# A DiT block on one core: the Fourier output product's sums and splits on VectorE and ScalarE, ordered behind the heads on both, and a quarter of the first sums on TensorE

## The chip, the cores and the metric

The kernel runs on one core of a Trainium2 chip. The metric is the device time of one execution in microseconds; lower is better. The core has five engines that each work through their own queue in order: PE (TensorE, matmuls), DVE (VectorE), ACT (ScalarE), POOL (GpSimd) and SP (SyncE, which here only starts DMAs). They meet at semaphores.

## The reference

One block of a diffusion transformer over 2048 tokens of width 1024, with 256 context tokens. What matters here, cut from the reference:

```python
m = jax.nn.silu(cond) @ w + b                       # ada_mod: six rows of modulation
hx = modulate(rms_norm(x, norm1_g[l]), sh1, sc1)
fx, qx, kx, vx = split_projection(hx @ w_in[l])
y_four = fourier_mix(fx)                            # real part of a 2-D FFT, 4 groups of 128
y_attn = neighbourhood_attention(qx, kx, vx, kc, vc, rpb[l])   # 8 heads
gates = jax.nn.sigmoid(h @ w_gate)
merged = g_f * (y_four @ w_fo) + g_a * (y_attn @ w_ao)
x = x + g1 * (merged @ w_o)
x = x + g2 * sqrelu_mlp(hx2, w_mlp1[l], w_mlp2[l])
```

The two places of the change are `silu(c) @ w_ada` for the first modulation, and `y_four @ w_fo`, the Fourier output product.

## The kernel before, in words

The program runs in stages, and most of them hand over by data: first the modulation sums and the first product of the input projection (to about 80 us of the profile), the rest of the projections (to about 835 us), the Fourier transforms (838 to 893), the attention heads (893 to 1230), the merge and output projection, and the MLP (1510 to the end).

**First stage.** For each of eight groups of 128 channels (k), `ada_sum` (L255) multiplies weight slices by silu(c) on DVE and adds them up in two accumulators; `ada_cols` (L268) then sums over partitions on TensorE with single-column matmuls: slices that DVE left are multiplied directly (L275), DVE's sum against ones (L276). PE_K (L605) says how many of the eight slices DVE takes for k = 2 and later; k = 0 and 1 are wholly DVE's. The result scales the tokens' channel group, which feeds the matmuls `ps_first`.

**Splits.** Matmuls that need more than one rounding take each operand as a high part and a low part: `split_on(eng_lo, hi, lo, src, eng_hi)` (L81) copies the source to `hi` on ACT, or on `eng_hi` where one is given (L85), and subtracts it from the source on `eng_lo` (L86).

**Heads.** There are 128 head steps: 4 head pairs (hp), 4 row blocks (rb), 4 column blocks (cb), 2 heads (h2). `block` (L1138) is one step: score matmuls `sc` (L1155, L1158), bias and minimum on DVE (L1164, output `s`, `m`), exponential on ACT (L1168), transposes `tp` on PE (L1177), high part `pH` on ACT (L1180), low part `pL` on DVE (L1185), matmuls `pv` (L1191) and their copy `yp` (L1194). Three steps are in flight, one stage apart. `behind("pe")`, `behind("dve")` and `behind("act")` keep each of these behind the last head instruction of its engine.

**Beside the heads** runs the generator `merge_fourier` (L1024 on), which computes y_four @ w_fo. It is pulled once or twice a step, under `issue_after(last_qk)` and `behind("dve")`; a scheduler then places its instructions by a model of when they are ready. In it: `load_w` fetches weight rows `wf` and their mirror `wm` (for half p = 0 on SP, for p = 1 on POOL's queue); the spectrum halves are fetched from DRAM `yF`; for each p the sum `ws` (POOL, L1055) and the difference `wf` (DVE, L1056) are made and split into wpH/wpL, wdH/wdL, and the spectrum into yaH/yaL, ybH/ybL (high parts on DVE, low parts on POOL but for wpL). Then the 4 rows at frequency 64 are loaded into `s64`, copied to `w64` and `a64` on ACT (L1076), and their low parts subtracted on POOL (L1078). The row product `pr` (L1092) of 14 matmuls is copied to `row`, turned by the transposes `puc` (L1098) and copied to `uc`. After that come 208 matmuls `pmf` (L1115), summed on DVE into `mo` (L1124, L1125) and stored. `pr`, `puc`, `pmf` and the transposes `ty` of the heads share one PSUM buffer. The generator goes on with the loads for the attention output product.

Of the kernel before, what the change touches and what calls it, by code (L numbers as in the profile page):

```python
# [8 lines left out]
F32 = mybir.dt.float32  # L9
# [5 lines left out]
ALU = mybir.AluOpType  # L15
# [44 lines left out]
def dit_block(ctx: ExitStack, tc: tile.TileContext, a, out, taps=None, upto=9):  # L60
# [42 lines left out]
    tT = [scratch(f"tT{c}", [16, 120, TCOL[c]]) for c in range(3)]  # L103


    yF = scratch("yF", [2, 2, 128, 1024])
    y64 = scratch("y64", [4, 1024])

    wfr = scratch("wfr", [4, 63, D])
# [492 lines left out]
    hx32 = [hx_room(f"first{o}").bitcast(F32R).rearrange("p o k t -> p (o k t)").rearrange("p (k t) -> p k t", t=512) for o in "HL"]  # L602
    first = [mmp.tile([128, 512], F32, tag="mm", name=f"ps_first{m}") for m in range(4)]
    sums, made = [], []
    PE_K = 4  # L605

    def first_sums(k):
        if k not in first_ada:
# [258 lines left out]
    def seq_dft(p):  # L867

        room = fb.tile([128, S], F32, tag="X", name="A1") if p else None
        for i in range(4):  # L870
            ps = seq_part(Gs[p][i], i, f"{p}_{i}")
            o = room[:, i * 512:(i + 1) * 512] if p else room_for(i, f"A{p}_{i}")
            if i == 0:
                add_alternating(o, ps, col[:, 2 * p:2 * p + 1])
            else:
                act.activation(o, ps, AF.Copy)
            act.dma_start(yF[p, i % 2, :, (i // 2) * 512:(i // 2 + 1) * 512], o)

    def seq_dft64():
        for i in (0, 2):  # L880
# [143 lines left out]
    def merge_fourier():  # L1024
# [14 lines left out]
        def load_w(p, fetch):  # L1039
# [5 lines left out]
                fetch(wm[o + 1:o + 64], wfr[2 * p + h])  # L1045
            return w, wm, t

        rows = load_w(0, fetch)
        for p in range(2):
            for x in range(2):  # L1050
                fetch(ys[x][1][:, p].bitcast(F32), yF[p, x])
        yield
        for p in range(2):
            w, wm, t = rows
            pool.tensor_tensor(t, w, wm, op=ALU.add)  # L1055
            dve.tensor_tensor(out=w, in0=w, in1=wm, op=ALU.subtract)  # L1056
            yield
            split_on(dve, ws[0][0][:, p], ws[0][1][:, p], t, dve)
            yield
            split_on(pool, ws[1][0][:, p], ws[1][1][:, p], w, dve)  # L1060
            if p == 0:
                rows = load_w(1, pool.dma_start)
            yield
            for x in range(2):
                hi, lo = (t[:, p] for t in ys[x])
                split_on(pool, hi, lo, lo.bitcast(F32), dve)
                yield

        w64, a64 = (mf.tile([68, D], F32R, tag=n, name=n) for n in ("w64", "a64"))
        c64 = mf.tile([68, 1], F32R, tag="c64", name="c64")  # L1070
        for r, src, lo in ((w64, raw(wf, 64 * D, [[128 * D, 4], [1, D]]), 64), (a64, y64, 32)):
            t = stage("s64", 68)
            pool.memset(t, 0.0)
            for o in (0, 32, 64):
                pool.dma_start(t[o:o + 4], src)
            act.activation(r, t, AF.Copy)  # L1076
            los = slice(lo, lo + 4)
            pool.tensor_tensor(r[los], t[los], r[los].bitcast(F32), op=ALU.subtract)  # L1078
# [23 lines left out]
        for m in range(8):  # L1102
            ms = slice(m * 128, (m + 1) * 128)
            o = [stage(f"mo{m}_{h}") for h in range(2)]
            pool.tensor_copy(o[1][:, 0:1], uc[:, m:m + 1])
            for par in range(2):
                ts = slice(par * 512, (par + 1) * 512)
                for x in range(2):
                    ps = mmp.tile([128, 512], F32, tag="mm", name=f"pmf{m}_{par}{x}")
                    (wH, wL), (yH, yL) = ws[x], ys[x]  # L1110
                    prods = [(l[:, p, ms], r[:, p, ts]) for p in range(2) for l, r in ((wH, yH), (wH, yL), (wL, yH))]
                    if x == 0:
                        prods.append((w64[:, ms], a64[:, ts]))
                    for i, (l, r) in enumerate(prods):
                        pe.matmul(ps, l, r, start=(i == 0), stop=(i == len(prods) - 1))  # L1115
                        count += 1
                        if count % 2 == 0 and i < len(prods) - 1:
                            yield
                    if x == 0:
                        u = mf.tile([128, 512], F32, tag="u", name=f"u{m}_{par}", bufs=2)  # L1120
                        act.activation(u, ps, AF.Copy)
                    else:
                        f = 1 - par
                        dve.tensor_tensor(out=view(o[0], par, [[2, 512]]), in0=u, in1=ps, op=ALU.subtract)  # L1124
                        dve.tensor_tensor(out=view(o[1], 1022 + par, [[-2, 512 - f]]), in0=u[:, f:], in1=ps[:, f:],  # L1125
                                          op=ALU.add)
                    if count % 2 == 0:
# [500 lines left out]
```

## Time and profile before

| | |
|---|---|
| median of 3 runs | 2784.8 us (2781.84 to 2786.85) |
| profiled execution | 2787.32 us |
| its span in the profile | 2785.5 us |
| granted TensorE clock, mean | 0.975 |
| PE busy | 2657.8 us (95%) |
| DVE, ACT, POOL busy | 1707.1, 1178.6, 371.2 us |
| chain that ended last | PE 77%, DVE 7%, DMA 7% |

All times below are on the clock of the profiled execution, from the start of its span. Busy time of PE contains the slowing by a lower granted clock; the mean of a group mixes it in. A row of the waits names what an engine waited for, in us. Instruction names leave buffer numbers out, so that w64 reads `w` and a64 reads `a`; a line can be that of a helper (L78, L85, L86).

### The profile page before, as it was taken

To read this page: it belongs to the slowest core of one execution; us is meant where nothing else is said; L and a number is where in the kernel's file an instruction comes from. 1 tells how busy PE (TensorE), PEld (TensorE's weight loads), DVE (VectorE), ACT (ScalarE), POOL (GpSimd) and SP (SyncE) were. 2 spreads that over 40 slices of the span, in tenths; PEclk is the share of its full clock that TensorE was granted. 3 is DMA by queue.
4 is the path that set the end of the run, shared out by engine and by line. 5 is a ranking of instruction groups with operands and counts; after the bars stand their busy time and mean duration, and the time that the engine had idled before them with its cause. 6 is when DMAs were issued, how large, how long until landed. Compare 5 with 4: busy or idle time off the path is not lost.

```text
span 2785.5 us, 41746 instructions
## 1 busy us (share of the span) xinstructions
PE 2657.8 (95%) x16257; PEld 1614.1 (58%) x16257; DVE 1707.1 (61%) x3366; ACT 1178.6 (42%) x2065; POOL 371.2 (13%) x496
## 2 busy tenths in 40 slices
PE   7899988999999699989999899999999999999999
PEld 6445656876647578878886344444444444444444
DVE  5656985255534768887666656655558456665536
ACT  4633226332323568863444644433333544433322
POOL 1111221012226745511000000000000000000000
PEclk8999999999998889999999999999999999999999
DMA  8487689452336455556656412111116211112102
GB/s 238 122 228 204 210 261 292 136 166 73 91 131 171 103 142 154 163 185 229 215 201 236 164 61 61 50 57 60 47 55 246 77 61 61 61 46 61 46 1 98
DMA packets 280862, 366.66 MB, mean 132 GB/s; under 512 B 38769, under 2 KB 217161, under 8 KB 276313
## 3 DMA queue, kind: packets, MB, share of 16 engines
q1 hardware_dynamic: 263913, 337.27, 38.7%
q0 software_dynamic: 11264, 16.76, 2.3%
q10 hardware_dynamic: 5488, 9.98, 1.0%
q8 instruction: 127, 2.08, 0.3%
q14 instruction: 70, 0.57, 0.1%
HBM read 277.83 MB, written 87.12 MB: 131 GB/s over the span
## 4 chain that ended last, share of the span: by engine, by line
PE 77%; DVE 7%; DMA 7%; ACT 1%; issue 1%; POOL 1%; SPq 0%; ACTq 0%; DVEq 0%; POOLq 0%
PE p L78 24%; PE pm L78 20%; PE ps_g L78 8%; PE po L78 6%; DMA w12m<-in_w_mlp 3%; PE pua L78 3%; PE ps_k L78 3%; PE tp L1177 2%; PE ps_v L78 2%; PE pv L1191 2%; PE pmf L1115 2%; PE sc L1155 1%; PE sc L1158 1%; DVE w1m L326 1%; DVE aaccg L264 1%
## 5 line engine op out<-in xcount | busy, mean ns | idle before, releaser
L78 PE MATMUL pm<-hc,wc 128*128 128x512 f16 x2688 | 589.1, 381 | 16.7 <-ACT p L1475 8.1
L78 PEld LDWEIGHTS <-wc 128*128 128x128 f16 x2688 | 264.2, 98 | 338.7 <-issue 25.6
L78 PE MATMUL p<-w2H,aH 128*128 128x512 f16 x1024 | 388.1, 379 | 0.5 <-ACT aH L1470 0.5
L78 PE MATMUL p<-w2H,aL 128*128 128x512 f16 x1024 | 388.1, 379 | 0.1
L78 PE MATMUL p<-w2L,aH 128*128 128x512 f16 x1024 | 388.1, 379 | 0.0
L1453 DVE TENSOR_TENSOR acc<-p,acc 128x512 f32<-128x512 f32 x224 | 154.7, 691 | 318.4 <-PE p L78 318.2
L78 PE MATMUL ps_g<-hx,w_g 128*128 128x512 f16 x1536 | 342.4, 380 | 0.7 <-ACT ot_f L419 0.7
L78 PEld LDWEIGHTS <-aH 128*128 128x128 f16 x2048 | 200.3, 98 | 242.2 <-ACT aH L1470 1.0
L1442 ACT ACTIVATE w2H<-w2s,msc 128x1024 f16<-128x1024 f32 x64 | 70.6, 1141 | 443.6 <-PE p L78 435.8
L78 PEld LDWEIGHTS <-w_g 128*128 128x128 f16 x1536 | 150.9, 99 | 171.3 <-issue 3.2
L78 PEld LDWEIGHTS <-hx 128*128 128x128 f16 x2304 | 226.1, 99 | 40.4 <-issue 6.7
L78 PEld LDWEIGHTS <-aL 128*128 128x128 f16 x1024 | 100.2, 98 | 121.3 <-DVE aL L1471 0.6
L947 POOL DMA_DIRECT2D bt<-tT x264 | 132.8, 510 | 66.0 <-DVE ri L1184 47.1
L1164 DVE CUSTOM_DVE_ANT_0 s<-sc,bt,qsc 128x736 f32<-128x736 f32 (+5 forms) x128 | 111.2, 869 | 44.8 <-PE sc L1158 40.3
L1443 DVE SCALAR_TENSOR_TENSOR w2L<-w2s,msc,w2H 128x1024 f16<-128x1024 f32 x64 | 80.7, 1282 | 92.6 <-ACT w2H L1442 92.6
L1442 ACT ACTIVATE wc<-ws,msc 128x512 f16<-128x512 f32 x128 | 91.1, 716 | 103.5 <-PE pm L78 101.5
L1185 DVE SCALAR_TENSOR_TENSOR pL<-tp,pH 128x640 f16<-128x640 f32 (+1 forms) x128 | 112.1, 876 | 24.5 <-ACT pH L1180 24.1
L419 ACT ACTIVATE ot_g<-ps_g,usc_g 128x512 f32<-128x512 f32 x64 | 43.7, 685 | 185.8 <-PE ps_g L78 180.6
L1168 ACT ACTIVATE s<-s,m 128x736 f32<-128x736 f32 (+5 forms) x128 | 104.4, 816 | 14.2 <-DVE m L1164 13.1
L78 PE MATMUL po<-wouH,mH 128*128 128x512 f32 x256 | 101.0, 398 | 7.2 <-DVE ga L1234 7.2
L1177 PE MATMUL tp<-ident,s 128*128 128x128 f32 x704 | 105.4, 285 | 2.2 <-ACT s L1168 2.2
L78 PE MATMUL po<-wouH,mL 128*128 128x512 f32 x256 | 100.5, 393 | 0.0
(494 smaller groups left out, 4724.1 us busy)
## 6 DMA issues: line engine op xcount, KB each, us to landing
w12m<-in_w_mlp SPq DMA_DIRECT2D x32, 1024.0 KB
w1r<-in_w_mlp SPq DMA_DIRECT2D x32, 1024.0 KB
w2s<-in_w_mlp SPq DMA_DIRECT2D x64, 512.0 KB
gT<-ot_g SPq DMA_DIRECT2D x64, 256.0 KB
hc<-hcd SPq DMA_DIRECT2D x14, 1024.0 KB
hcd<-ho SPq DMA_DIRECT2D x42, 256.0 KB
x<-in_x SPq DMA_DIRECT2D x20, 512.0 KB
ws_g<-in_w_branch_gate SPq DMA_DIRECT2D x16, 512.0 KB
```

Of the source, the lines that this page charges most:

```text
L78: last_mm[0] = pe.matmul(ps, l, r, start=(start and i == 0), stop=(stop and i == n - 1))
L419: act.activation(o, ps, func, scale=scale)
L947: load_(t[i * 16:(i + 1) * 16, :, off + j0 * w:off + (j0 + 8) * w], raw(tT[ct], (2 * hp * 15 + dr) * w, [[120 * w, 16], [15 * w, 2], [1, 8 ...
L1115: pe.matmul(ps, l, r, start=(i == 0), stop=(i == len(prods) - 1))
L1164: tail["dve"] = dve.tensor_tensor_reduce(out=s[:, :n], in0=sc, in1=bias, op0=ALU.add, op1=ALU.min, scale=qsc[:, 4:5], scalar=3.0e38, accum ...
L1168: tail["act"] = act.activation(s[:, :n], s[:, :n], AF.Exp, bias=m1[:, 0:1], scale=-1.0, accum_out=m1[:, 1:2])
L1177: tail["pe"] = pe.transpose(tp[:, i * 128:(i + 1) * 128], s[:, o:o + 128], ident)
L1185: tail["dve"] = dve.scalar_tensor_tensor(out=pL[:, :c], in0=tp[:, :c], scalar=PTOP, in1=pH[:, :c], op0=ALU.mult, op1=ALU.subtract)
L1191: tail["pe"] = pe.matmul(pv, p_[:nk, i * 128:(i + 1) * 128], vv[:nk, h2 * 128 + o:h2 * 128 + o + 64], start=(j == 0 and i == 0), stop=(j = ...
L1442: act.activation(hi, src, AF.Copy, scale=scale)
L1443: dve.scalar_tensor_tensor(out=lo, in0=src, scalar=scale, in1=hi, op0=ALU.mult, op1=ALU.subtract)
L1453: dve.tensor_tensor(out=o, in0=x, in1=y, op=ALU.add)
```

## The change

It has three parts.

1. PE_K goes from 4 to 6: for k = 2 to 7, DVE sums six of the eight weight slices, and TensorE multiplies two instead of four directly.
2. In the Fourier output product, the sum `ws` goes from POOL to DVE, all eight high parts of weights and spectrum go from DVE to ACT, all low parts that POOL made go to DVE, and so do the two low parts of w64 and a64. Differences stay on DVE. The s64 tiles are allocated, cleared and loaded at the start of the generator, in the buffers of `u`, which become 1024 columns wide. DRAM `yF` becomes four tensors.
3. The pulls of the generator stand behind the last head instruction on ACT too, not on DVE alone.

```diff
@@ yF
-    yF = scratch("yF", [2, 2, 128, 1024])
+    yF = [[scratch(f"yF{p}{x}", [128, 1024]) for x in range(2)] for p in range(2)]
@@ first stage
-    PE_K = 4
+    PE_K = 6
@@ merge_fourier
+        s64 = []
+        for src in (raw(wf, 64 * D, [[128 * D, 4], [1, D]]), y64):
+            t = mf.tile([68, D], F32, tag="u", name="s64", bufs=2)
+            pool.memset(t, 0.0)
+            for o in (0, 32, 64):
+                pool.dma_start(t[o:o + 4], src)
+            s64.append(t)
...
-            pool.tensor_tensor(t, w, wm, op=ALU.add)
+            dve.tensor_tensor(out=t, in0=w, in1=wm, op=ALU.add)
             dve.tensor_tensor(out=w, in0=w, in1=wm, op=ALU.subtract)
             yield
-            split_on(dve, ws[0][0][:, p], ws[0][1][:, p], t, dve)
-            yield
-            split_on(pool, ws[1][0][:, p], ws[1][1][:, p], w, dve)
+            split_on(dve, ws[0][0][:, p], ws[0][1][:, p], t)
             if p == 0:
                 rows = load_w(1, pool.dma_start)
             yield
+            split_on(dve, ws[1][0][:, p], ws[1][1][:, p], w)
+            yield
             for x in range(2):
                 hi, lo = (t[:, p] for t in ys[x])
-                split_on(pool, hi, lo, lo.bitcast(F32), dve)
+                split_on(dve, hi, lo, lo.bitcast(F32))
                 yield
...
-        for r, src, lo in ((w64, raw(wf, 64 * D, [[128 * D, 4], [1, D]]), 64), (a64, y64, 32)):
-            t = stage("s64", 68)
-            pool.memset(t, 0.0)
-            for o in (0, 32, 64):
-                pool.dma_start(t[o:o + 4], src)
+        for r, lo in ((w64, 64), (a64, 32)):
+            t = s64.pop(0)
             act.activation(r, t, AF.Copy)
             los = slice(lo, lo + 4)
-            pool.tensor_tensor(r[los], t[los], r[los].bitcast(F32), op=ALU.subtract)
+            dve.tensor_tensor(out=r[los], in0=t[los], in1=r[los].bitcast(F32), op=ALU.subtract)
             yield
...
-                        u = mf.tile([128, 512], F32, tag="u", name=f"u{m}_{par}", bufs=2)
+                        u = mf.tile([128, D], F32, tag="u", name=f"u{m}_{par}", bufs=2)[:, :512]
@@ step
-            with tc.issue_after(last_qk[0].ins), behind("dve"):
+            with tc.issue_after(last_qk[0].ins), behind("dve"), behind("act"):
                 next(filler, None)
```

The new lines move the numbering: what is line n before stands at n + 4 from the middle of the generator on (L1164 becomes L1168, L1092 becomes L1096). The scheduler places the instructions anew. Three places follow, each before and after.

**DVE, the second half (p = 1) of the weight sums.** Names end in row block and column block, so `s_..,m_3_2` is the score instruction of rb 3, cb 2. Before:

```order
L1164 ISA s_9102,m_3_2_10460<-sc_3_2_10455,bt_9001,qsc 128x640
L1164 ISA m_3_2_10460 128x1
L1184 RECIPROCAL ri_3_1_10462<-m_3_1_10366 128x1
L1056 TENSOR_TENSOR wf_9364<-wf_9364,wm_9365 128x1024
L85 CAST wpH<-ws_9366 128x1024
L85 CAST wdH<-wf_9364 128x1024
L86 TENSOR_TENSOR wpL<-ws_9366,wpH 128x1024
L1185 SCALAR_TENSOR_TENSOR pL_3_1_10453<-tp_3_1_10446,pH_3_1_10452 128x640
L1164 ISA s_9103,m_3_2_10509<-sc_3_2_10504,bt_9001,qsc 128x640
```

After (here rb 1, cb 2 and 3):

```order
L1188 RECIPROCAL ri_1_1_9683<-m_1_1_9588 128x1
L86 TENSOR_TENSOR yaL<-yaL,yaH 128x1024
L1063 TENSOR_TENSOR ws_9319<-wf_9317,wm_9318 128x1024
L1189 SCALAR_TENSOR_TENSOR pL_1_1_9674<-tp_1_1_9666,pH_1_1_9673 128x768
L1168 ISA s_9095,m_1_3_9731<-sc_1_3_9726,bt_8988,qsc 128x616
L1168 ISA m_1_3_9731 128x1
L1188 RECIPROCAL ri_1_2_9733<-m_1_2_9638 128x1
L86 TENSOR_TENSOR ybL<-ybL,ybH 128x1024
L1064 TENSOR_TENSOR wf_9317<-wf_9317,wm_9318 128x1024
L1189 SCALAR_TENSOR_TENSOR pL_1_2_9724<-tp_1_2_9716,pH_1_2_9723 128x768
L86 TENSOR_TENSOR wpL<-ws_9319,wpH 128x1024
L1168 ISA s_9096,m_1_3_9777<-sc_1_3_9772,bt_8988,qsc 128x616
```

The p = 1 work stood together in rb 3; it now stands in rb 1, some fourteen steps earlier, and in pieces between the heads' `s`, `ri` and `pL`.

**PE, the row product `pr`.** `w_9755` and `w_9756` are w64. Before, directly behind the scores of rb 3, cb 2, the rest of the first row half (`pr_9869`) and the second (`pr_9878`):

```order
L78 MATMUL pr_9869<-wpH,cH_9864 1x512
L78 MATMUL pr_9869<-wpL,cH_9864 1x512
L78 MATMUL pr_9869<-wpH,cL_9865 1x512
L1092 MATMUL pr_9869<-w_9755,c_9757 1x512
L78 MATMUL pr_9878<-wpH,cH_9860 1x512
L78 MATMUL pr_9878<-wpL,cH_9860 1x512
L78 MATMUL pr_9878<-wpH,cL_9861 1x512
L78 MATMUL pr_9878<-wpH,cH_9864 1x512
L78 MATMUL pr_9878<-wpL,cH_9864 1x512
L78 MATMUL pr_9878<-wpH,cL_9865 1x512
L1092 MATMUL pr_9878<-w_9755,c_9757 1x512
L1098 MATMUL puc<-ident,row 128x1 x8
```

After, within the transposes `tp` of rb 2, cb 0:

```order
L1181 MATMUL tp_2_0_9947<-ident,s_9093 128x128 x2
L78 MATMUL pr_9860<-wpH,cL_9852 1x512
L78 MATMUL pr_9860<-wpH,cH_9855 1x512
L78 MATMUL pr_9860<-wpL,cH_9855 1x512
L78 MATMUL pr_9860<-wpH,cL_9856 1x512
L1096 MATMUL pr_9860<-w_9756,c_9758 1x512
L1181 MATMUL tp_2_0_9947<-ident,s_9093 128x128 x4
```

The first half of `pr` moved from behind the scores of step 28 (steps counted from 0) into the transposes of rb 2, cb 0; the second half follows one step later, and the `pmf` matmuls that followed `pr` start in rb 2, cb 1.

**PE, the sums of one k in the first stage.** `ads` is the modulation column, `ps_first` the first product. Before:

```order
L201 MATMUL tp_4_380<-ident,xh_163 128x128
L275 MATMUL ads_367<-sil,sparec 128x1 x4
L276 MATMUL ads_367<-ones,aaccs_319 128x1
L275 MATMUL ads_367<-sil,sparec 128x1 x4
L276 MATMUL ads_367<-ones,aaccs_319 128x1
L78 MATMUL ps_first_183<-firstH,w_first_200 128x512
L78 MATMUL ps_first_183<-firstL,w_first_200 128x512
L78 MATMUL ps_first_183<-firstH,w_first_200 128x512
L78 MATMUL ps_first_184<-firstH,w_first_200 128x512
```

After:

```order
L78 MATMUL ps_first_189<-firstL,w_first_207 128x512
L78 MATMUL ps_first_189<-firstH,w_first_207 128x512
L275 MATMUL ads_411<-sil,sparer 128x1 x2
L276 MATMUL ads_411<-ones,aaccs_362 128x1
L275 MATMUL ads_411<-sil,sparer 128x1 x2
L276 MATMUL ads_411<-ones,aaccs_362 128x1
L78 MATMUL ps_first_186<-firstH,w_first_301 128x512
L78 MATMUL ps_first_187<-firstH,w_first_301 128x512
L78 MATMUL ps_first_188<-firstH,w_first_305 128x512
```

Each half has two direct matmuls instead of four. The matmuls of `ps_first` with firstL that followed the sums now stand ahead of the next k's.

More of the change, by code (lines that the diff above doesn't have):

```diff
@@ L876, in seq_dft @@
                 act.activation(o, ps, AF.Copy)
-            act.dma_start(yF[p, i % 2, :, (i // 2) * 512:(i // 2 + 1) * 512], o)
+            act.dma_start(yF[p][i % 2][:, (i // 2) * 512:(i // 2 + 1) * 512], o)
     def seq_dft64():
@@ L1050, in merge_fourier @@
             for x in range(2):
-                fetch(ys[x][1][:, p].bitcast(F32), yF[p, x])
+                fetch(ys[x][1][:, p].bitcast(F32), yF[p][x])
         yield
```

## The prediction

> **What bounds the kernel now.** I read the shares by engine, then the busy time by stretch, then the chain of waits through the worst stretch, then the rows of the engines that it names.
>
> ```profile
> PE 2657.8 (95%) x16257; PEld 1614.1 (58%) x16257; DVE 1707.1 (61%) x3366; ACT 1178.6 (42%) x2065; POOL 371.2 (13%) x496
> ```
>
> TensorE has work for 2657.8 of 2785.5 us: only its 128 idle us, or work taken off it, can pay. The stretches (span; length; busy PE, PEld, DVE, ACT, POOL with counts; granted PE clock; DMA share; GB/s):
>
> ```profile
> 900.00:920.00 20.00, 15.84 (x195) 13.29 (x193) 14.61 (x31) 12.47 (x31) 12.47 (x15) 0.82 0.95 250
> 920.00:940.00 20.00, 15.19 (x185) 12.55 (x184) 18.98 (x38) 13.02 (x28) 15.34 (x15) 0.83 0.40 103
> 940.00:960.00 20.00, 19.61 (x299) 17.07 (x295) 19.71 (x45) 18.30 (x41) 13.75 (x23) 1.00 0.27 61
> 960.00:980.00 20.00, 3.78 (x8) 0.71 (x9) 4.08 (x7) 1.75 (x3) 14.98 (x20) 0.54 0.10 20
> ...
> 1000.00:1160.00 160.00, 159.11 (x1934) 130.22 (x1933) 132.21 (x296) 127.61 (x288) 80.74 (x164) 1.00 0.56 157
> ```
>
> One hole stands out: in 960 to 980 PE is busy 3.78 us while POOL is busy 14.98. At 920 to 940 the bound is DVE (18.98 of 20, PE 15.19 at clock 0.83). After 1000 PE is full. The chain through the hole (start, length, engine, tile, line), and its wait (total, times, longest):
>
> ```profile
> 960.62 1.12 DVE wf L1056
> 961.74 0.60 DVE wpH L85
> 962.35 0.61 DVE wdH L85
> ...
> 963.03 3.25 POOL wdL L86
> ...
> 968.25 3.85 POOL bt L947 x8
> ...
> 974.76 2.34 POOL w L1078
> 977.14 0.60 PE pr L1092
> ...
> 978.41 2.72 PE pr L78 x6
> ...
> 982.23 1.02 PE puc L1098 x8
> ...
> PE pr L1092 <- POOL w L1078: 12.0, 1, 12.0
> ```
>
> The row product `pr` needs `w64`, which leaves POOL's queue only behind wdL, the s64 loads and the bias loads `bt`; TensorE's next head steps stand behind `pr`. DVE's score instruction opens each step, which dates the damage:
>
> ```profile
> 912.60 0.86 DVE L1164 CUSTOM_DVE_ANT_0 s<-sc,bt,qsc 128x616 f32<-128x616 f32 x1 [3.83 <-PE sc L1158]
> ...
> 937.67 0.86 DVE L1164 CUSTOM_DVE_ANT_0 s<-sc,bt,qsc 128x616 f32<-128x616 f32 x1
> ...
> 959.65 0.88 DVE L1164 CUSTOM_DVE_ANT_0 s<-sc,bt,qsc 128x640 f32<-128x640 f32 x1
> 987.65 0.89 DVE L1164 CUSTOM_DVE_ANT_0 s<-sc,bt,qsc 128x640 f32<-128x640 f32 x1 [1.06 <-PE sc L1158]
> ...
> 1028.08 0.98 DVE L1164 CUSTOM_DVE_ANT_0 s<-sc,bt,qsc 128x736 f32<-128x736 f32 x1 [0.49 <-PE sc L1158]
> ...
> 1074.42 0.79 DVE L1164 CUSTOM_DVE_ANT_0 s<-sc,bt,qsc 128x544 f32<-128x544 f32 x1
> ```
>
> Counted from 0 these are steps 8, 16, 28, 29, 44 and 64. Step 28 to 29 takes 28.0 us; steps 16 to 28 take 21.98, so 1.83 each.
>
> **First stage.** Here PE's full time holds the small sums (start, length; the last row is a stretch as above):
>
> ```profile
> 43.99 0.95 PE L275 MATMUL ads<-sil,sparec 128*128 128x1 f32 x8
> 44.80 0.36 PE L276 MATMUL ads<-ones,aaccs 128*128 128x1 f32 x2
> 45.02 1.03 PE L275 MATMUL ads<-sil,sparec 128*128 128x1 f32 x8
> 45.91 0.36 PE L276 MATMUL ads<-ones,aaccs 128*128 128x1 f32 x2
> 50.99 0.95 PE L275 MATMUL ads<-sil,sparer 128*128 128x1 f32 x8
> ...
> 47.00 0.87 DVE L264 SCALAR_TENSOR_TENSOR aaccs<-awts,sil,aaccs 128x256 f32<-128x256 f32 x2
> ...
> 43.90:50.90 7.00, 7.00 (x39) 6.01 (x38) 2.67 (x8) 1.45 (x2) 0.00 (x0) 0.76 0.97 346
> ```
>
> One k lasts 7.00 us (43.99 to 50.99), and L275 holds 0.81 + 0.89 = 1.70 of it, start to next start. PE_K 6 halves these matmuls for k = 2 to 7: 0.85 us less PE in each of the five k from 3 on, 4.25; at k = 2, where PE still waits for data, 0 to 0.85, and I take 0.75. DVE gets two more multiply-adds per k, 0.87 us by its row, beside 2.67 busy of 7.00: hidden. Without that cover it would cost 0.87 x 6 = 5.2 and nothing would be gained. **Term: -5.0, from 0 to -5.1.** It reaches the end only if later stages start earlier with it; one stretch could keep it back:
>
> ```profile
> 250.00:430.00 180.00, 166.26 (x1137) 113.23 (x1135) 154.55 (x419) 54.68 (x124) 37.38 (x36) 0.97 0.79 236
> ...
> 347.51 7.21 DMA w12m<-in_w_mlp
> 354.74 2.29 DVE w1m L326
> 357.06 7.31 DMA w12m<-in_w_mlp
> ```
>
> PE idles 13.7 us there. But DMA at 0.79 is not full, and in the chain each load of w12m follows the DVE reduction that frees its buffer (354.74 + 2.29 = 357.03), so the loads start from the work's own progress, and I let the stretch shift as a whole.
>
> **Heads, up to step 16.** Prices of the operations moved (start, length):
>
> ```profile
> 908.08 0.68 DVE L85 CAST yaH<-yaL 128x1024 fp32r<-128x1024 f32 x1
> ...
> 917.84 3.89 DVE L1056 TENSOR_TENSOR wf<-wf,wm 128x1024 f32<-128x1024 f32 x1
> ...
> 960.53 1.21 DVE L1056 TENSOR_TENSOR wf<-wf,wm 128x1024 f32<-128x1024 f32 x1
> ...
> 969.08 1.06 ACT L1076 ACTIVATE w<-s 68x1024 fp32r<-68x1024 f32 x1 [10.36 <-DMA s<-in_w_fourier_out]
> ```
>
> The same subtraction took 1.21 us alone and 3.89 beside POOL's sums. After the change POOL has none, so each two-input instruction on DVE costs 1.21: two sums, two differences, eight low parts (four weights, four `ya`/`yb`), two small ones for w64 and a64 (1024 columns on 4 partitions: 0 to 1.21, I take 1.21 by columns). That is 14 x 1.21 = 16.9 us. Before, DVE had 3.89 + 1.21, two low parts of 1.21 and eight casts of 0.68: 13.0. So DVE gains 4 us of work, ACT eight copies of about 1.06 (8.5), and POOL loses its sums.
>
> By the order, five of the 14 come ahead of step 8 (sum, difference, wpL, wdL, yaL). In the trace DVE waited 3.83 before step 8, from 908.77, after a cast that leaves: 908.77 - 0.68 + 5 x 1.21 = 914.1 for step 8, 1.5 later than 912.60. ybL follows (1.21); with 1.83 a step, step 10 starts at 914.1 + 3.7 + 1.2 = 919. Six more steps and the eight instructions between steps 13 and 16 give 919 + 11.0 + 9.7 = 939.7. The copies stand on ACT ahead of the exponentials of steps 5 to 8 and 12 to 15. If DVE's additions hide them, 939.7 stands; if each of the second group's six also delays its step by 1.06, it is 946. **I take 942.5** for step 16, 4.8 later than 937.67: nearer the low end, because DVE receives an addition in the same steps.
>
> **Heads, from step 16.** Both orders hold the same Fourier matmuls again by step 44 (64 of `pmf`). Their price, warm:
>
> ```profile
> 995.33 1.64 PE pmf L1115 x7
> ```
>
> 0.234 each. Steps 44 to 64 took 46.34 us with 50 `pmf`: (46.34 - 11.7) / 20 = 1.73 for a step alone. From 16 to 44 this gives 28 x 1.73 = 48.4, plus 64 x 0.234 = 15.0, plus 14 `pr` at 0.234 = 3.3, plus `puc` 1.0, plus 2 for the two `pr` copies and the `puc` copy through the one product buffer: 69.7. Step 44 then starts at 942.5 + 69.7 = 1012.2 instead of 1028.08: **-15.9, from -21 (939.7, hand-offs hidden) to -8 (946 and another 4 us of hand-offs)**. I count -15, since the s64 and second weight loads now share the full DMA of 900 to 920 (share 0.95): 0 to 2 us late for the Q loads. Were w64 late again, up to 16 us of this would return.
>
> Nothing else moves on the path: POOL's six s64 DMAs come earlier in the same number, and the split of yF only lets the first loads go before the last write. The wider `u` tiles and `behind("act")` are no instructions of their own. **Sum: -5 - 15 = -20.** The profiled execution took 2787.3 us, so 2767.3; the median of the runs shown is 2784.8, so about **2765**.
>
> **Rivals.**
>
> *The clock comes along.* The first stage runs at a granted 0.76. If shorter sums lift it to 1.00, a k of 6.15 us shrinks by up to 24%, 1.5 us, so five k give up to 7; at -6 in all the result is 2759. For it: full use at 0.76 in every k. Against: the same matmuls would still be there in half number. [...]
>
> *Half of it is absorbed.* Either DVE and ACT, both over 18 of 20 us at 940 to 960, bound steps 16 to 44 too (a third us a step, 28 steps: 9 back), or the first stage's 5 us end in the stretch 250 to 430, whose chain then has DMA ahead of PE. Then -11 to -15, and the middle is 2772.
>
> *The hole moves.* It does not do what it says if `pr` now waits on w64's new place, DVE's queue behind wdL, as long as on POOL's: -5 + 4 = 2784. Against: the order puts w64 before wdL and `pr` a step later.
>
> *The other side: slower.* In-order queues make each low part wait for its high part on ACT. Place: steps 4 to 16. If each of ten pairs exposes its copy and ACT's remaining step (1.06 + 1.7 = 2.8, where the step's score queues behind the low part on DVE), step 16 comes 28 us after 942.5, at 970, step 44 at 1040; with -5 from the first stage the time is 2785 + 12 - 5 = 2792. It decides from step 16 at 963 (no gain left). Against: ACT was busy 13.02 of 20 in the stretch at 920, so the copies have room. [...]
>
> **Numbers.** Forecast as summed 0.50; the clock comes along 0.13; half absorbed 0.20; the hole moves 0.10; slower 0.07. A change under 0.2% (5.6 us) cannot be told from none. Faster: 0.50 + 0.13 + 0.20 = 0.83, and 0.01 of the moved hole; same 0.09; slower 0.07. The range runs from 2755 (clock at -11 in the first stage, heads at -19) to 2781 (first term lost, and half of the heads' low end); the hole's 2784 and the slower case are left out.
>
> **What would show it.** Right: step 16 at about 937 (942.5 less the 5), step 28 to 29 under 3 us, PE over 18 of 20 us from 945 on, no TENSOR_TENSOR on POOL in that stretch, every f32 two-input DVE row near 1.21; L275 at half count and a k of about 6.15 us. Wrong: a wait of `pr` on DVE or ACT of several us; step 16 after 945; a start of the Fourier transforms less than 4 us earlier; DVE full and PE below 18 after step 16.

## The result

The changed kernel takes **2763.48 us** (median of 4 runs, 2761.16 to 2767.06) against 2784.81 for the kernel before (median of 4, 2781.84 to 2786.85). The ratio is 0.9925, 95% interval 0.9908 to 0.9943: 21 us faster, with 16 to 26 inside the interval. The forecast was 2765. The profiled execution has a span of 2765.3 us.

The page of the changed kernel, its busy row:

```profile
PE 2643.2 (96%) x16209; PEld 1601.2 (58%) x16209; DVE 1716.2 (62%) x3380; ACT 1185.0 (43%) x2073; POOL 346.4 (13%) x486
```

Its stretches, with the columns of the stretches in the prediction. The first row is the first stage, the others the heads:

```profile
40.00:60.00 20.00, 19.16 (x117) 16.32 (x115) 16.71 (x48) 10.31 (x15) 4.78 (x5) 1.00 0.86 285
900.00:920.00 20.00, 15.34 (x166) 11.94 (x164) 18.05 (x36) 14.15 (x29) 11.12 (x21) 0.83 0.94 218
920.00:940.00 20.00, 12.18 (x136) 9.65 (x136) 16.29 (x25) 14.96 (x30) 3.47 (x7) 0.83 0.24 65
940.00:960.00 20.00, 20.00 (x238) 15.65 (x237) 14.14 (x31) 15.18 (x34) 10.38 (x23) 1.00 0.25 63
960.00:980.00 20.00, 20.00 (x246) 16.57 (x247) 16.50 (x39) 16.10 (x38) 13.59 (x27) 1.00 0.58 159
```

The hole is gone: PE is busy all 20 us at 960 to 980, where it was busy 3.78. The first stage runs at a granted clock of 1.00; the same stretch of the kernel before:

```profile
40.00:60.00 20.00, 20.00 (x105) 17.10 (x103) 9.83 (x27) 6.28 (x10) 2.01 (x2) 0.74 0.58 182
```

VectorE's score instructions of steps 0, 16, 28, 29 and 44 in the changed kernel:

```profile
887.41 0.76 DVE L1168 CUSTOM_DVE_ANT_0 s<-sc,bt,qsc 128x520 f32<-128x520 f32 x1 [2.60 <-PE sc L1162]
...
937.46 0.86 DVE L1168 CUSTOM_DVE_ANT_0 s<-sc,bt,qsc 128x616 f32<-128x616 f32 x1
...
967.69 0.88 DVE L1168 CUSTOM_DVE_ANT_0 s<-sc,bt,qsc 128x640 f32<-128x640 f32 x1
970.75 0.88 DVE L1168 CUSTOM_DVE_ANT_0 s<-sc,bt,qsc 128x640 f32<-128x640 f32 x1
...
1004.46 0.98 DVE L1168 CUSTOM_DVE_ANT_0 s<-sc,bt,qsc 128x736 f32<-128x736 f32 x1 [0.42 <-PE sc L1162]
```

Step 28 to 29 takes 3.1 us instead of 28.0. Steps 0 to 44 take 117.1 us (887.41 to 1004.46). In the kernel before they took 135.1, from the row below to 1028.08:

```profile
893.01 0.76 DVE L1164 CUSTOM_DVE_ANT_0 s<-sc,bt,qsc 128x520 f32<-128x520 f32 x1 [2.60 <-PE sc L1158]
```

So the heads give 18.0 us, and they start 5.6 us earlier: 23.6 at step 44, of which 20.2 are left in the span. In between, the lead is not constant. Matching the two traces instruction by instruction (start before less start after) gives 12.1 us at the end of the first stage, 12.7 at 384 us, 7.9 at 493, 7.8 at 838 and 5.6 at 893.

### The profile page after: what moved, and what is told of

The parts are those of the page before. It is cut to its first block, busy times and chain, and to the rows that moved or that the text cites. A ratio compares the mean times of both kernels' runs of the same rounds, so it can differ in the third digit from the quotient of the medians.

```text
span 2765.3 us, 41669 instructions
## 1 busy us (share of the span) xinstructions
PE 2643.2 (96%) x16209; PEld 1601.2 (58%) x16209; DVE 1716.2 (62%) x3380; ACT 1185.0 (43%) x2073; POOL 346.4 (13%) x486
## 4 chain that ended last, share of the span: by engine, by line
PE 76%; DMA 9%; DVE 6%; issue 2%; ACT 1%; POOL 1%; SPq 0%; ACTq 0%; DVEq 0%; POOLq 0%
PE p L78 24%; PE pm L78 20%; PE ps_g L78 8%; PE po L78 6%; DMA w12m<-in_w_mlp 3%; PE pua L78 3%; PE ps_k L78 3%; PE tp L1181 2%; PE ps_v L78 2%; PE pmf L1119 2%; PE pv L1195 2%; PE sc L1159 1%; DMA wm<-in_wmask 1%; PE sc L1162 1%; DMA Q<-qH 1%
## 5 line engine op out<-in xcount | busy, mean ns | idle before, releaser
L1168 DVE CUSTOM_DVE_ANT_0 s<-sc,bt,qsc 128x736 f32<-128x736 f32 (+5 forms) x128 | 111.2, 869 | 37.3 <-PE sc L1162 33.8
```

The lines of the kernel that those rows point to most:

```text
L1168: tail["dve"] = dve.tensor_tensor_reduce(out=s[:, :n], in0=sc, in1=bias, op0=ALU.add, op1=ALU.min, scale=qsc[:, 4:5], scalar=3.0e38, accum ...
```

## The experiments

The table puts the traces of the experiments side by side with those of the two kernels. Lead is how much earlier than in the kernel before an instruction starts, at the end of the first stage (74 us), at 493 us, at 838 us and at step 0 of the heads (893 us); negative is later.

| kernel | lead 74 | 493 | 838 | step 0 | steps 0 to 44 | step 28 to 29 | ratio to before (95%) |
|---|---|---|---|---|---|---|---|
| before | 0 | 0 | 0 | 0 | 135.1 | 28.0 | 1 |
| changed | 12.1 | 7.9 | 7.8 | 5.6 | 117.1 | 3.1 | 0.9925 (0.9908 to 0.9943) |
| first sums alone | 12.4 | 11.2 | 13.0 | 14.4 | 136.0 | 27.5 | 0.9969 (0.9952 to 0.9985) |
| Fourier part alone | 3.0 | 1.7 | 0.5 | -0.5 | 119.7 | 3.1 | 0.9955 (0.9937 to 0.9974) |
| padded | 2.1 | 2.7 | 2.9 | 7.2 | 119.3 | 3.1 | 0.9932 (0.9916 to 0.9949) |
| PE_K 8 | 5.9 | 6.9 | 5.3 | 9.5 | 122.5 | 3.1 | 0.9924 (0.9905 to 0.9944) |
| PE_K 5 | 4.9 | -1.0 | -1.6 | -4.6 | 118.9 | 3.1 | 0.9935 (0.9911 to 0.9959) |
| not behind ACT | 10.9 | 4.9 | 7.0 | 7.0 | 130.1 | 3.1 | 0.9945 (0.9928 to 0.9962) |
| high parts on DVE | 10.7 | 9.5 | 9.3 | 9.4 | 120.9 | 3.1 | 0.9914 (0.9893 to 0.9935) |
| low parts on POOL | 10.8 | 12.9 | 13.3 | 13.1 | 121.2 | 13.8 | 0.9952 (0.9938 to 0.9966) |
| s64 early alone | 0.6 | -1.1 | 1.1 | 0.6 | 125.8 | 15.9 | 0.9987 (0.9975 to 0.9998) |
| yF stores on SP | 10.6 | 11.4 | 10.5 | 5.6 | 118.7 | 3.1 | 0.9937 (0.9920 to 0.9953) |
| s64 early and sum | 2.4 | -0.2 | -1.3 | -1.5 | 115.5 | 3.1 | 0.9926 (0.9909 to 0.9942) |
| the same with PE_K 6 | 10.7 | 7.2 | 6.0 | 6.8 | 115.3 | 3.1 | 0.9928 (0.9912 to 0.9944) |

The leads and steps of a kernel are from one profiled execution, its ratio from several runs. The leads between 74 us and step 0 vary by 5 us and more between kernels whose first stages lead by the same 11 to 12, and single runs of one kernel lie up to 14 us apart. So mechanisms are read from the traces of the place itself, and a ratio only says whether the whole moved. The profiled execution of PE_K 5 is its longest, 2780.24 us against 2766 to 2769 for the other three, so its leads are those of an unusual one.

### Are the two parts independent?

First sums alone:

```diff
-    PE_K = 4
+    PE_K = 6
```

> The kernel before with PE_K 6 and nothing else. Theory A (fewer single-column matmuls also free the clock): one k of the first stage takes about 4.6 us at a granted clock of 1.00, as in the changed kernel, the lead at 75 us is 12 us, and the loads of w12m between 390 and 500 us take 4 of it back; the hole of 28 us in the heads stays. End: 5 to 8 us faster, 2777 to 2780. Theory B (only the matmuls' own time goes, and the clock in the changed kernel was chance): one k about 6.15 us at 0.76 to 0.80, lead at 75 us about 5, end 2779 to 2784.

The Fourier part alone (an edit of the changed kernel):

```diff
-    PE_K = 6
+    PE_K = 4
```

> The changed kernel with PE_K back at 4: the Fourier part alone. Theory A (the two parts are independent and add): start of the heads as before (893), step 16 about 5 us later than in the changed kernel (943), step 28 to 29 under 4 us, 13 to 18 us faster: 2767 to 2772. Rival: the gain of the heads needs the earlier start (loads of Q and the weights land at a time of their own): step 16 at 937 as in both kernels and a gain of 20 us or more.

The first sums alone are 8.6 us faster by their ratio (median 2775.70, 1.3 us earlier than the expected range), the Fourier part 12.5 (median 2775.96, 4 us later than its range): together 21.1, and the change as a whole gives 21. That agrees with parts that add, but weakly: the intervals run from 4 to 13 and from 7 to 18 us, and the last kernel of the section on the hole, where the first sums add nothing that can be measured, speaks against it. The places are as in theory A: the hole stays at 27.5 us in the one and falls to 3.1 in the other. In this execution the first sums led by 12.4 us at 74 us and by 14.4 at step 0, so the loss of 4 us in the loads of w12m, which was expected of them, is not a property of the first sums.

### What the first stage gained

In the changed kernel, the sums of one k (start, length):

```profile
40.33 0.50 PE L275 MATMUL ads<-sil,sparec 128*128 128x1 f32 x4
...
40.92 0.58 PE L275 MATMUL ads<-sil,sparec 128*128 128x1 f32 x4
...
44.90 0.50 PE L275 MATMUL ads<-sil,sparer 128*128 128x1 f32 x4
```

One k takes 4.57 us (40.33 to 44.90), not the 6.15 of the forecast. The padded kernel puts as many single-column matmuls back as there were, against zeros, and leaves the longer sums on VectorE (the lines that make the column of zeros `zer` are left out):

```diff
             for k in range(nk, KT):
                 pe.matmul(ps[:, i:i + 1], wt[:, k, bs], sil[:, k:k + 1], start=(k == nk), stop=False)
+                if nk == 6:
+                    pe.matmul(ps[:, i:i + 1], wt[:, k, bs], zer, start=False, stop=False)
```

> The changed kernel with four more single-column matmuls per k for k = 2 to 7, against a column of zeros, so TensorE has as many as before while VectorE still sums six slices. Theory A: one k returns to about 7.0 us at clock 0.76; at 75 us the lead of 12 is gone; end 5 to 8 us slower than the changed kernel, 2769 to 2772. Theory B (the order of the matmuls or the sums on VectorE, not their number, moved the clock): one k about 5.4 us at clock 1.00 (4.57 and 0.82 for four more), end about 2766.

Its stretch and the first of its padding matmuls in two successive k:

```profile
40.00:60.00 20.00, 20.00 (x105) 17.25 (x104) 11.87 (x32) 5.08 (x9) 2.75 (x3) 0.76 0.49 158
...
42.00 0.36 PE L279 MATMUL ads<-zer,sparec 128*128 128x1 f32 x2
...
49.01 0.36 PE L279 MATMUL ads<-zer,sparer 128*128 128x1 f32 x2
```

A k is back at 7.01 us and the clock at 0.76, with the longer sums in place. The order of the matmuls is that of the kernel before again in most of these k, with the transposes last; but the k from 34.83, 7.03 us at 0.76, has the matmuls of `ps_first` still in the order of the changed kernel. So it is the number of single-column matmuls that decides the clock here: theory A, as far as the stage goes. The end did not follow. The padded kernel takes 2765.07, no later than the changed kernel within its interval, and not the 2769 to 2772 that was expected. Its lead was 10 us smaller at 74 us, 5 smaller at 838, and 1.6 larger at step 0: it lost nothing in the loads and gained 4.3 us in the Fourier transforms, where the changed kernel lost 2.2.

PE_K 5 asks whether the clock moves by steps.

```diff
-    PE_K = 6
+    PE_K = 5
```

> The changed kernel with PE_K 5. Theory A (the clock is a step: it either stays at 1.00 or falls to 0.76): one k is either about 5.0 us at clock 1.00 (4.57 and 0.41 for one more slice in each half) or about 6.6 at 0.76 (7.00 less 0.43), nothing between. Rival (the clock follows the share of single-column matmuls smoothly): about 5.8 us at 0.85 to 0.92. End between 2761 and 2772 in either case, since other stages scatter by 5 us.

```profile
40.00:60.00 20.00, 20.00 (x122) 17.51 (x120) 12.81 (x37) 6.96 (x11) 3.40 (x3) 0.94 0.60 184
...
44.01 0.73 PE L275 MATMUL ads<-sil,sparec 128*128 128x1 f32 x6
...
48.98 0.73 PE L275 MATMUL ads<-sil,sparer 128*128 128x1 f32 x6
```

A k takes 4.97 us, the 5.0 of the step at full clock, and the later ones 5.01 and 5.01; from 44 us on the clock is 1.00, and the 0.94 of the stretch comes from the k before, 6.66 us at 0.62. Four direct matmuls a column (7.01 us), three (5.0) and two (4.57): the second saving is 0.43, the work of one more slice, the first is 2.0. In these k the step lies between four and three.

Four slices do not always bring the lower clock. One k of the Fourier part alone ran at 1.00, and so did one of s64 early and sum; the k behind them were slow again, at 0.76 in the former. The first row is that k of the Fourier part alone; after it comes one k of the kernel before in two stretches, cut where its 512-column matmuls slow down:

```profile
35.63:41.07 5.44, 5.44 (x38) 4.88 (x37) 3.64 (x12) 1.45 (x2) 0.00 (x0) 1.00 1.20 294
...
43.99:46.90 2.91, 2.91 (x25) 2.80 (x24) 0.59 (x3) 0.00 (x0) 0.00 (x0) 1.00 1.09 339
46.90:50.99 4.09, 4.09 (x14) 3.21 (x13) 2.09 (x6) 1.45 (x2) 0.00 (x0) 0.58 0.87 351
```

With four slices a k takes 5.44 us at full clock and 7.01 at 0.76, so the clock is worth 1.57 us a k, and the two slices that go 0.87 (5.44 to 4.57). And it is not the single-column matmuls that slow down: all 20 of them stand in the first stretch, at 1.00. The 512-column matmuls of `ps_first` behind them do, from 0.23 to 0.43 us from start to start.

In the kernel before, read in half-microsecond stretches from 43 to 59 us, the granted clock is 0.50 or 1.00, and a value between the two stands only in a stretch in which it changes: 1.00 from 43.5 to 46.5 us, 0.50 from 47.0 to 50.0, 1.00 from 50.5 to 53.5, 0.50 from 54.0 to 57.0. So the 0.76 of a k is a mean of full and half clock, two fixed values with a step between them. In the changed kernel every such stretch from 40 to 52 us has 1.00. What brings the lower value is not shown: PE is busy 20.00 of 20 us at 40 to 60 us both in the kernel before, at 0.74, and in the padded one, at 0.76. The runs show that more single-column matmuls bring the slow stretches (0.76 padded, 1.00 in the changed kernel); why they do stays open.

PE_K 8 leaves TensorE nothing but the sums against ones.

```diff
-    PE_K = 6
+    PE_K = 8
```

> The changed kernel with PE_K 8: VectorE sums all eight slices. If TensorE bounds a k, it goes from 4.57 to about 3.75 us and five k give 4 us at 75 us. If VectorE takes over (its busy time per k would be near 4.4 us), a k stays at 4.4 to 5 us and nothing is gained or up to 2 us lost. Either way at most half reaches the end, since the loads of w12m take a part back: 2760 to 2766.

```profile
40.00:60.00 20.00, 13.26 (x70) 10.83 (x69) 18.42 (x54) 8.12 (x12) 5.39 (x5) 0.98 0.86 285
```

VectorE is busy 18.42 of 20 us and PE 13.26: VectorE has taken over. The lead at 74 us is 5.9 instead of 12.1, so this is worse for the stage by 6 us, more than the 2 expected; the end (2764.21) does not show it, as in the padded kernel: by step 0 the lead is 9.5.

### What the hole was made of

> The kernel before with the s64 tiles loaded at the start, nothing else. Theory A (two causes in GpSimd's queue, w64 and the second half's sum): w64 is ready before step 16, but the product still waits for the second half's weights, which stand at step 28: step 28 to 29 falls from 28 to 10 to 18 us, and the end is 8 to 14 us earlier than before, 2771 to 2777. Rival B (w64 alone): step 28 to 29 under 5 us, 20 us or more earlier. Rival C (s64 never mattered, the sum's queue did): 28 us stays, no gain.

s64 early alone (the kernel before; the line that widens `u` is left out):

```diff
+        s64 = []
+        for src in (raw(wf, 64 * D, [[128 * D, 4], [1, D]]), y64):
+            t = mf.tile([68, D], F32, tag="u", name="s64", bufs=2)
+            pool.memset(t, 0.0)
+            for o in (0, 32, 64):
+                pool.dma_start(t[o:o + 4], src)
+            s64.append(t)
         rows = load_w(0, fetch)
...
-            t = stage("s64", 68)
-            pool.memset(t, 0.0)
-            for o in (0, 32, 64):
-                pool.dma_start(t[o:o + 4], src)
+            t = s64.pop(0)
```

GpSimd's low part of w64 and its sum for the second half; steps 28 and 29 on VectorE, and between them the difference of the second half, which overwrites an operand of the sum and so stands behind it; what `pr` waits for; and the time from step 28 to 29 in three stretches:

```profile
921.49 2.36 POOL L1082 TENSOR_TENSOR w<-s,w 4x1024 fp32r<-4x1024 f32 x1
...
952.39 2.39 POOL L1062 TENSOR_TENSOR ws<-wf,wm 128x1024 f32<-128x1024 f32 x1
...
962.65 0.88 DVE L1168 CUSTOM_DVE_ANT_0 s<-sc,bt,qsc 128x640 f32<-128x640 f32 x1
...
963.53 1.21 DVE L1063 TENSOR_TENSOR wf<-wf,wm 128x1024 f32<-128x1024 f32 x1
...
978.52 0.88 DVE L1168 CUSTOM_DVE_ANT_0 s<-sc,bt,qsc 128x640 f32<-128x640 f32 x1 [1.05 <-PE sc L1162]
...
PE pr L78 <- DVE wpH L85: 2.8, 1, 2.8
...
962.65:967.13 4.48, 0.59 (x1) 0.08 (x1) 4.43 (x7) 0.00 (x0) 1.49 (x2) 0.73 0.08 16
967.13:974.39 7.26, 5.59 (x18) 1.83 (x18) 0.00 (x0) 1.35 (x3) 5.60 (x8) 0.50 0.14 28
974.39:978.52 4.13, 4.12 (x29) 3.59 (x30) 0.82 (x2) 3.61 (x9) 2.18 (x5) 0.52 0.38 99
```

w64 is ready at 924, 53 us earlier than before, and `pr` still does not run: it needs the second half's weights, and these stand at step 28 in VectorE's queue. Step 28 to 29 falls from 28.0 to 15.9 us, as theory A had it. So w64's place in GpSimd's queue was less than half of the hole. Nor are the other 15.9 us all a wait for weights: PE waits 3.9 us for them (2.8 for wpH, 1.1 for wpL). Then the rest of the row product, its copies and its transposes run one behind the other with no head step among them, 7.26 us at a granted clock of 0.50, and the heads' own matmuls start again at 0.52. In the changed kernel most of the same `pr` stands among the transposes of the heads at 940 to 944 us, where the clock is 1.00. So the place in the order costs twice, as a wait and as a stretch that runs alone and slowly. The heads win 9.3 us, but the end only about 4 (ratio 0.9987, median 2783.33), where 8 to 14 were expected: its lead of 9.9 at step 44 was 6.2 at step 120.

Low parts on POOL: the changed kernel with the sums and low parts back on GpSimd. The edit is the lines of the change reversed, here two of them:

```diff
-            dve.tensor_tensor(out=t, in0=w, in1=wm, op=ALU.add)
+            pool.tensor_tensor(t, w, wm, op=ALU.add)
...
-                split_on(dve, hi, lo, lo.bitcast(F32))
+                split_on(pool, hi, lo, lo.bitcast(F32))
```

> The changed kernel with the sums and low parts back on GpSimd; early s64, high parts on ScalarE and the ordering stay. Theory A (the hole is GpSimd's queue: the second half's sum ws stands there behind the bias loads): the second half's difference and splits stand at step 28 again, step 28 to 29 takes 10 to 20 us, and the end is 6 to 14 us later than the changed kernel, 2770 to 2778. Rival B (the hole was w64 alone, which is early here): step 28 to 29 under 5 us, end within 4 us of the changed kernel.

```profile
930.66 2.36 POOL L1063 TENSOR_TENSOR ws<-wf,wm 128x1024 f32<-128x1024 f32 x1
...
946.72 0.88 DVE L1168 CUSTOM_DVE_ANT_0 s<-sc,bt,qsc 128x640 f32<-128x640 f32 x1
...
947.60 1.21 DVE L1064 TENSOR_TENSOR wf<-wf,wm 128x1024 f32<-128x1024 f32 x1
...
960.56 0.88 DVE L1168 CUSTOM_DVE_ANT_0 s<-sc,bt,qsc 128x640 f32<-128x640 f32 x1 [1.06 <-PE sc L1162]
```

13.8 us and 2773.11, as theory A expected. The end can't be put down to the hole alone, though: steps 0 to 16 take 42.6 us here against 50.1, steps 0 to 44 only 4.2 more than in the changed kernel, and of a lead of 27.0 us at step 44 another 5.5 go by step 120, which is not explained. Nor was the reason exact: the sum is finished at 933.0, and VectorE takes up the difference at 947.6. The trace shows no wait that holds it for these 14 us, only its place in VectorE's queue, behind step 28. That order is written when the program is built, presumably by a reckoning that knows GpSimd's long queue; how it is reckoned was not tried. Moving the sum to VectorE changed the order, not only the wait.

That leaves the smallest edit that should do it: s64 early, and the two sums on VectorE, with everything else of the Fourier part as in the kernel before.

```diff
-            pool.tensor_tensor(t, w, wm, op=ALU.add)
+            dve.tensor_tensor(out=t, in0=w, in1=wm, op=ALU.add)
```

> The kernel before with the s64 tiles loaded at the start and the two sums ws on VectorE; high parts stay on VectorE, low parts on GpSimd, no ordering behind ScalarE, PE_K 4. Theory A (the hole was two places in GpSimd's queue, w64 and the second half's sum): no step takes over 5 us between 16 and 44, steps 0 to 44 take 117 to 122 us instead of 135, and the end is 12 to 18 us earlier than before, 2768 to 2773, as with the whole Fourier part. Rival B (the low parts on GpSimd matter as much: wdL of the second half is late, and VectorE's instructions beside GpSimd's take 3 us and more): steps 0 to 44 take 125 us or more.

Steps 28 and 29 of it, then the sum and a cast of the first half, the same two of the second, and a subtraction on GpSimd beside the second cast:

```profile
973.30 0.88 DVE L1168 CUSTOM_DVE_ANT_0 s<-sc,bt,qsc 128x640 f32<-128x640 f32 x1 [0.21 <-PE sc L1162]
976.39 0.88 DVE L1168 CUSTOM_DVE_ANT_0 s<-sc,bt,qsc 128x640 f32<-128x640 f32 x1
...
904.76 1.22 DVE L1062 TENSOR_TENSOR ws<-wf,wm 128x1024 f32<-128x1024 f32 x1
908.59 0.69 DVE L85 CAST wpH<-ws 128x1024 fp32r<-128x1024 f32 x1
...
933.99 1.67 DVE L1062 TENSOR_TENSOR ws<-wf,wm 128x1024 f32<-128x1024 f32 x1
938.88 2.83 DVE L85 CAST wpH<-ws 128x1024 fp32r<-128x1024 f32 x1
...
938.37 2.79 POOL L86 TENSOR_TENSOR ybL<-ybL,ybH 128x1024 fp32r<-128x1024 f32 x1
```

Theory A holds in full: steps 0 to 44 take 115.5 us, the shortest so far, and the end is 2768.86 with a PE_K of 4. VectorE's instructions for the second half are longer (the cast 2.83 us beside GpSimd's subtraction instead of 0.69, the sum 1.67 instead of 1.22 in a stretch, 920 to 940 us, in which GpSimd is busy 19.72 of 20), but it has fewer instructions, and the low parts on GpSimd are in time. With PE_K 6 added to it:

> The kernel before with three edits: s64 loaded at the start, the sums ws on VectorE, PE_K 6. Theory (these are the whole gain, and the high parts on ScalarE, the low parts on VectorE and the ordering behind ScalarE add nothing): steps 0 to 44 take 115 to 119 us, one k 4.6 us, the end as the changed kernel or up to 4 us earlier, 2759 to 2766. Rival (the rest of the change carries part of the gain): 2767 or later.

2766.89 over 6 runs, ratio 0.9928, interval 0.9912 to 0.9944: not told apart from the changed kernel's 0.9925, though the median lies at the border between the two expectations. Steps 0 to 44 take 115.3 us, so nothing of the heads' gain needs the other edits. Nor can it be told apart from the kernel without PE_K 6, at 0.9926: the first sums, worth 8.6 us alone, add nothing here that these runs can measure. In the profiled executions they do add something (a lead at step 44 of 26.6 us against 18.1), but that is one execution of each.

### What the other edits do

Without the ordering behind ScalarE:

```diff
-            with tc.issue_after(last_qk[0].ins), behind("dve"), behind("act"):
+            with tc.issue_after(last_qk[0].ins), behind("dve"):
```

> The changed kernel without the ordering behind the heads on ScalarE. By its order the four copies of the spectrum's high parts then stand on ScalarE ahead of the first head's exponential, and each needs a load of yF that lands 10 to 15 us after the heads start. Theory (ScalarE's queue is in order, so the heads wait for the loads): step 4 starts 8 to 15 us later than in the changed kernel, and the end is 5 to 12 us later, 2769 to 2775. Rival (the ordering is idle, since the loads land in time): within 3 us of the changed kernel.

ScalarE's queue at the start of the heads in this kernel:

```profile
896.83 1.06 ACT L83 ACTIVATE yaH<-yaL 128x1024 fp32r<-128x1024 f32 x1 [10.05 <-DMA yaL<-yF]
...
903.33 1.06 ACT L83 ACTIVATE ybH<-ybL 128x1024 fp32r<-128x1024 f32 x1 [1.12 <-DMA ybL<-yF]
...
905.70 0.73 ACT L1172 ACTIVATE s<-s,m 128x520 f32<-128x520 f32 x1
```

ScalarE stands 10.05 us for a load with the first exponential behind it. Step 4 starts 18 us later than in the changed kernel (expected 8 to 15), steps 0 to 44 take 130.1, and the end is 10 us later by the medians (2773.49) and 6 by the ratios, whose intervals overlap: the direction of the theory, shown by the trace rather than by the end. So once the high parts are on ScalarE, the ordering is needed.

High parts on VectorE (three `split_on` calls with `dve` for the high part):

```diff
-            split_on(dve, ws[0][0][:, p], ws[0][1][:, p], t)
+            split_on(dve, ws[0][0][:, p], ws[0][1][:, p], t, dve)
```

> The changed kernel with the eight high parts on VectorE (0.69 us each there) instead of ScalarE (1.06). Theory (VectorE bounds steps 4 to 16, ScalarE's copies are hidden): VectorE has 5.5 us more, step 16 comes 4 to 6 us later, the end 3 to 6 us later, 2767 to 2770. Rival (the wait of each low part on ScalarE's copy bounds these steps): step 16 comes up to 3 us earlier and the end with it, 2760 to 2764.

From step 0, step 16 comes 2.4 us later than in the changed kernel (52.5 us after it instead of 50.1), and steps 0 to 44 take 120.9, 3.9 more. That is the direction of the theory, that VectorE bounds these steps, but step 16 moves by less than half of the added 5.5 us, and less than the 4 to 6 expected. At the end nothing is left of it: 2761.08 instead of 2767 to 2770, ratio 0.9914, inside the changed kernel's interval. Its heads began 3.8 us earlier in the profiled execution.

### Where the transforms lose

> The changed kernel with the eight stores of yF issued by the Sync engine instead of ScalarE. Theory (in the Fourier transforms ScalarE stood behind a store that waited for an earlier load, up to 7 us, with the next high part behind it): the lead over the kernel before grows by about 4 us between 838 and 893 us, as in the padded kernel, where it shrank by 2.2 in the changed kernel; the end comes 3 to 6 us earlier, 2758 to 2762. Rival (the loads of the heads, now behind waiting stores on the Sync queue, land later): step 4 starts 3 us or more later relative to step 0 and nothing is gained.

```diff
-            act.dma_start(yF[p][i % 2][:, (i // 2) * 512:(i // 2 + 1) * 512], o)
+            sp.dma_start(yF[p][i % 2][:, (i // 2) * 512:(i // 2 + 1) * 512], o)
```

```profile
858.75 0.60 ACT L876 ACTIVATE A<-psq 128x512 f32<-128x512 f32 x1 [4.67 <-DMA yF<-A]
```

Refuted. With the stores on the Sync engine, ScalarE does not stand behind their issue, but its next copy into `A` waits 4.67 us for an earlier store to land and free the buffer; with a second such wait that makes 10.1 us, against 4.6 in the changed kernel. The lead shrinks by 4.9 us between 838 and 893 us instead of growing by 4, and the end is 2770.69. Nor did the rival happen as it was put: from step 0, step 4 is 0.9 us later, not 3.

One thing goes with a short or a long stretch of transforms, the granted clock. From the instruction that stands at 838 us in the kernel before, to step 0, in the changed kernel, the padded one and this one:

```profile
830.20:887.41 57.21, 53.65 (x272) 44.11 (x270) 20.77 (x58) 11.84 (x32) 37.27 (x60) 0.82 0.57 158
...
835.10:885.85 50.75, 49.62 (x271) 40.69 (x270) 21.02 (x58) 11.80 (x32) 34.76 (x55) 0.90 0.61 173
...
827.50:887.45 59.95, 54.52 (x271) 45.20 (x270) 20.75 (x58) 11.93 (x32) 37.47 (x60) 0.80 0.56 151
```

57.2 us at 0.82, 50.8 at 0.90 and 60.0 at 0.80; PE_K 8 has 50.8 at 0.90, and the kernel before 55.0 at 0.84. PE is busy for 91 to 98% of each of the three. Why two of the kernels (padded, PE_K 8) had the higher clock and the others did not is left open; the loads for the heads share the DMA there, and the order of loads and stores differs between these kernels.

## Why the prediction was right, and where it was not

**The first stage: the step was mis-sized, and so was its way to the end.** -5.0 was forecast with a k of 6.15 us at the old clock; 12.1 us were won at a k of 4.57. The matmuls that went were worth what the sum had, 0.87 us a k against 0.85. The term that it put at nothing was the clock: it went from 0.76 to 1.00, worth 1.57 us a k. This is the mechanism of the rival that got a chance of 0.13 and priced it at 1.5, and it held in every kernel with PE_K 6 that was not padded, with leads of 10.6 to 12.4 us at 74 us. Then "I let the stretch shift as a whole" failed: between 384 and 493 us, in the loads of w12m, 4.8 us went, and 2.2 in the transforms. The waits show the first, by groups over the same work (after the last bar: idle before, and what ended it). First the kernel before, 384 to 493 us, then the changed one, 371.3 to 485.1:

```profile
L328 ACT ACTIVATE w12m<-w12m 128x2048 f32<-128x2048 f32 x14 | 26.7, 1910 | 22.5 <-DMA w12m<-in_w_mlp 18.3 <-DMA gT<-ot_g 4.2
L326 DVE TENSOR_REDUCE w1m<-w12m 128x1 f32<-128x2048 f32 x9 | 20.6, 2284 | 9.2 <-DMA w12m<-in_w_mlp 9.1
```

```profile
L328 ACT ACTIVATE w12m<-w12m 128x2048 f32<-128x2048 f32 x14 | 26.7, 1910 | 23.9 <-DMA w12m<-in_w_mlp 23.9
L326 DVE TENSOR_REDUCE w1m<-w12m 128x1 f32<-128x2048 f32 x9 | 20.6, 2285 | 12.4 <-DMA w12m<-in_w_mlp 12.4
```

VectorE stands 3.2 us longer before its reductions and ScalarE 1.4 longer before its squares of w12m, which follow them: 4.6 of the 4.8. Why the loads came later is not shown; the DMA share of the two stretches is 0.91 and 0.86. At step 0 the lead was 5.6, near the 5.0 forecast, by luck: two errors cancelled. Since the first sums alone kept 14.4 us in their profiled execution, the loss is no fixed price.

**The heads to step 16: right.** Step 16 was forecast at 942.5 less 5, and came at 937.46. From step 0 it took 50.1 us instead of 44.7: 5.4 later, forecast 4.8. The price of the moved instructions held to a hundredth (groups between 885 and 1000 us):

```profile
L1063 DVE TENSOR_TENSOR ws<-wf,wm 128x1024 f32<-128x1024 f32 x2 | 2.4, 1221 | 0.2 <-DMA wm<-wfr 0.2
L1082 DVE TENSOR_TENSOR w<-s,w 4x1024 fp32r<-4x1024 f32 x1 | 1.2, 1217 | 0.0
L83 ACT ACTIVATE wpH<-ws 128x1024 fp32r<-128x1024 f32 x2 | 2.1, 1060 | 0.4 <-DVE ws L1063 0.4
```

Four rows of 1024 columns cost VectorE as much as 128: choosing the high end by columns was right.

**From step 16: right, 2.7 us too careful.** 69.7 was forecast and 67.0 measured. The slack of 2 us for the hand-offs of `pr` was not needed: the heads' transposes stand on both sides of it, and PE is busy 20.00 of 20 us at 940 to 960. The heads gave 18.0, the sum had 15. Of the signs that were named, step 28 to 29 came at 3.06 us, just over "under 3", and the k at 4.57 instead of 6.15.

**What the hole was: half right.** The prediction put it on w64 behind GpSimd's queue. With w64 out of the way the hole was still 15.9 us: 3.9 of waiting for the second half's weights, placed at step 28 of VectorE's queue, and 7.3 of the row product behind them, alone and at a clock of 0.50; the rest is the steps' own work at a low clock. The change moved both, so the sum came out. The forecast did see that place move, in the order, but did not price it as a cause.

**The rivals.** Half absorbed: the loss did come in the loads of w12m, 3.3 of the 4.8 us by the end of the stretch that the rival named, but beside a larger gain. The hole did not move. Slower: the copies on ScalarE did not hold up the steps, and the kernel without the ordering shows what they cost where they do: 13 us from step 0 to 44.

**The sum.** -5 - 15 = -20 forecast; 5.6 + 18.0 = 23.6 at step 44, and 21.3 by the medians.

## What to carry to other kernels

When a stall hangs on one late operand, look for the next operand of the same instruction before pricing the cure: here the second kept 16 of 28 us, and by the trace it was late only by its written place in a queue. Count with a wait also the work that it pushes into a stretch of its own: 7 of these 16 us were the row product alone, at a clock of 0.50. Of a change with many edits, two (an early load and two sums) gave 0.9926, as much of the whole change's 0.9925 as could be measured. A gain in an early stage is only worth what the load-bound stages behind it leave of it (12.1 us at 74 us in the changed kernel were 7.9 at 493, behind the loads of w12m), so price it at them too.

## What the runs showed that was not expected

- Single-column matmuls decided the granted clock of a stage: four direct slices a column gave 0.76 in a k once running, three and two gave 1.00, and a k fell from 7.01 to 5.0 and 4.57 us. The padded kernel brought 0.76 back. What slowed was not these matmuls but the 512-column ones behind them, 0.43 us from start to start instead of 0.23.
- The time between first stage and heads scattered by 5 us and more from one kernel's execution to another's: a lead of 12.1 shrank to 5.6 in the changed kernel, and one of 12.4 grew to 14.4 with the first sums alone. It hid every difference under some 5 us at the end. In the transforms it went with the granted clock, from 60.0 us at 0.80 to 50.8 at 0.90.
- The same cast on VectorE took 2.83 us beside a GpSimd subtraction and 0.69 without; a two-input sum 1.67 and 1.22. A difference took 3.89 in the one case that the prediction quoted, beside two low parts on GpSimd (915.96 to 920.64 us), not its sums, and 1.21 with GpSimd idle.
